# Sums over the rows of w_ada on TensorE, with the weights stationary, in one layer of a hybrid decoder

## The chip, the core and the metric

The kernel runs on one core of one Trainium2 chip. The metric is the device time of one execution in microseconds (us), the median of several runs.

## What is computed

One layer of a decoder trunk on a sequence of 1024 tokens of 1024 channels, conditioned by a vector c. From c come six vectors of 1024 (shift, scale and gate, for the mixing part and for the feed-forward part), and they are what the change is about:

```python
c_act = jax.nn.silu(c)
ada = c_act @ w_ada[l] + b_ada[l]                  # (1024) @ (1024 x 6144)
sh_m, sc_m, g_m, sh_f, sc_f, g_f = jnp.split(ada, 6, axis=-1)
h = modulate(rms_norm(x), sh_m, sc_m)              # h * (1 + sc) + sh
proj = h @ w_in[l]                                 # z for RWKV-7, u for S5
...
x = x + g_m[:, None, :] * mix                      # after the output projection
h = modulate(rms_norm(x), sh_f, sc_f)
ffn = (jax.nn.silu(h @ ffn_w_gate[l]) * (h @ ffn_w_up[l])) @ ffn_w_down[l]
x = x + g_f[:, None, :] * ffn
```

w_ada has 1024 rows and 6144 columns in float32, 25 MB. Everything is float32; large products are made as three products of a high and a low part (float32r).

## The kernel before

Channels lie on the 128 partitions, tokens on the free axis. The engines are TensorE (PE, with its weight loads, PEld), VectorE (DVE), ScalarE (ACT) and GpSimd (POOL); nearly all loads and stores are issued by SyncE (SP) from one queue. The program is written as generators that are woven into each other, and a scheduler then sets the order of the instructions on each engine from a model of their times, so that an edit can move instructions that it does not touch. Within an engine, and within SP's queue, the order is fixed: an instruction that waits holds back those behind it.

The stages, with their times in the profile: the startup (0 to 106 us), in which x is normalized, transposed by products with diagonals (`ptr`, `transpose_x`, L337), modulated (`hT`, `modulate`, L346) and multiplied by the columns of w_in for u (`pu`, `u_mm`, L363); the rest of the input projection (`pz`), the S5 recurrence and the preparation of RWKV (to about 440 us); the RWKV recurrence in chunks (`p`, `chunk`, L1037) woven with the gate of S5 (`pglu`, `s5_glu`, L763) and the triangular solve (`solve`, L980); the output projection of the first half of the tokens (`po`, `outproj`, L1271), to about 662 us; then the feed-forward network (`pgate`, `pup`, `pdn`, `ffn`, L1343) by halves, woven with what is left of RWKV.

The six vectors are made in blocks of 128 columns. `cact` holds silu(c) as eight columns, one for each block of 128 rows of w_ada. `ada_load` (L278) loads the 1024 rows of n blocks of columns in four tiles `wada`, each with two blocks of rows. `ada_acc` (L287) makes a running sum `acc` over the eight blocks of rows, elementwise: a product with the scalar `cact[:, 0]` (L293), then seven multiply-adds on DVE (L295), or, for some pieces, a product on ACT (L297) and a sum on POOL (L298). What is left is a sum over the partitions, and `ada_cols` (L301) makes it with one product for each block of columns, weights `acc`, one moving column of ones (`pac<-ones,acc`, L304), and then adds b_ada into `mod` (L305).

- Parts 0 and 1 (shift and scale of the mixing part) are made in the startup, in two halves of four blocks of columns (L528 to L557): the first half before the channels 0 to 511 are modulated, the second before the channels 512 to 1023.
- Parts 2 and 3 are made by `ada_steps` (L816, `adg`, L1239) in eight pieces of two blocks beside the recurrence and the gate of S5; every second piece has its sums on ACT and POOL.
- Parts 4 and 5 are made in eight pieces (`adl`, L1417), all on DVE, beside the output projection. The norm of the feed-forward part (`norm_f`, L1316) needs parts 3 and 4, the gate row (`bcast_gate`, L1245) part 5.

## Time and profile before

| | us |
|---|---|
| median of 3 runs | 1602.5 |
| lowest, highest | 1602.16, 1603.44 |
| span of the profiled execution | 1598.3 |

The profile's page gives the profiled execution's span, from its first to its last instruction, and no other time of it; the median of the runs stands 4.2 us above the span.

How to read it: the page gives the busy time of each engine and its share of the span, then the span in 40 slices with the busy tenths and TensorE's granted clock (in tenths of full speed; full is 2.4 GHz, one half of it 1.2 GHz, and a slice's figure is the mean over it). A chain of waits leads back from the last instruction; its shares tell which work stood on the path. Groups of instructions have their count, their busy time, the mean of one, and the idle time of the engine before them with what ended it. A float32 product appears as two records of PE and two weight loads.

### The profile page before, as it was taken

What the parts mean: (1) busy time and instruction counts of PE and PEld (TensorE: products, weight loads), DVE (VectorE), ACT (ScalarE), POOL (GpSimd) and SP (SyncE); (2) the same over time, 40 slices, a digit from 0 to 9 for tenths busy, and PEclk for the clock granted to TensorE, in tenths of its full rate; (3) what the DMA queues carried; (4) which work ended last, traced back from release to release, by engine and by line L of the source; (5) the groups of instructions that cost most, each with busy time, mean ns of one, the idle gap of its engine ahead of it and who ended that gap; (6) DMA issues with size and microseconds to landing.
All of it is one profiled execution on the core that took longest, in us unless ns stands there. A gap on an engine that the chain in (4) does not pass through costs nothing.

```text
span 1598.3 us, 23239 instructions
## 1 busy us (share of the span) xinstructions
PE 1416.4 (89%) x9167; PEld 1146.8 (72%) x9167; DVE 988.7 (62%) x1687; ACT 551.9 (35%) x881; POOL 540.9 (34%) x452
## 2 busy tenths in 40 slices
PE   3897798897958878698999999899997999999997
PEld 3675576776747756576777777677786888888885
DVE  5959458889686889854448855345626433433335
ACT  4341234344245653233225422224443222222223
POOL 4358344443053333145000003400251254444543
PEclk9897999999878989799999999899999999999999
DMA  9424674353454356353223224422831433232331
GB/s 277 146 79 143 171 233 152 109 134 100 93 161 129 122 177 196 115 116 97 66 67 113 86 88 106 97 68 68 222 104 50 137 93 105 81 105 92 99 99 53
DMA packets 266220, 189.78 MB, mean 119 GB/s; under 512 B 71670, under 2 KB 237184, under 8 KB 266112
## 3 DMA queue, kind: packets, MB, share of 16 engines
q1 hardware_dynamic: 264624, 186.65, 39.7%
q8 instruction: 72, 1.18, 0.3%
q0 software_dynamic: 816, 0.57, 0.2%
q10 hardware_dynamic: 672, 1.08, 0.2%
q14 instruction: 36, 0.29, 0.1%
HBM read 159.20 MB, written 31.16 MB: 119 GB/s over the span
## 4 chain that ended last, share of the span: by engine, by line
PE 56%; DVE 22%; DMA 8%; issue 5%; POOL 5%; ACT 2%; SPq 2%; DVEq 0%; POOLq 0%; ACTq 0%
PE pup L268 14%; PE pgate L268 13%; PE pdn L268 13%; PE pz L268 3%; DMA wada<-in_w_ada_dram 3%; PE p L1051 3%; DVE acc L295 2%; POOL XU L997 2%; POOL stmp L995 2%; PE pu L365 2%; PE po L1303 2%; DVE zo L864 1%; DVE stmp L995 1%; PE pA L951 1%; DVE XU L997 1%
## 5 line engine op out<-in xcount | busy, mean ns | idle before, releaser
L268 PE MATMUL pdn<-wd,act 128*128 128x512 f32 x1056 | 269.1, 397 | 0.7 <-DVE x L1352 0.6
L268 PE MATMUL pup<-h,hl_up 128*128 128x512 f32 x1056 | 268.6, 397 | 0.2 <-ACT hl_up L131 0.2
L268 PE MATMUL pgate<-h,hl_g 128*128 128x512 f32 x1056 | 264.1, 396 | 1.2 <-ACT hl_g L131 1.2
L1352 DVE TENSOR_TENSOR x<-pdn,x 128x512 f32<-128x512 f32 x176 | 119.0, 688 | 185.8 <-PE pdn L268 185.2
L268 PEld LDWEIGHTS pup<-h,hl_up 128*128 128x128 f32 x1056 | 198.1, 189 | 45.9 <-issue 2.6
L268 PEld LDWEIGHTS pdn<-wd,act 128*128 128x128 f32 x1056 | 196.6, 189 | 47.4 <-DVE x L1352 2.1
L268 PEld LDWEIGHTS pgate<-h,hl_g 128*128 128x128 f32 x1056 | 196.6, 188 | 47.4 <-issue 3.6
L268 PE MATMUL pz<-hT,hl_z 128*128 128x256 f32 (+1 forms) x1008 | 184.7, 340 | 37.0 <-ACT zt L859 20.8
L268 PEld LDWEIGHTS pz<-hT,hl_z 128*128 128x128 f32 x1008 | 154.7, 202 | 63.6 <-ACT zt L859 25.5
L1387 DVE TENSOR_TENSOR rawd<-rawd,gfb 128x1024 f32<-128x1024 f32 x44 | 54.9, 1248 | 101.2 <-DMA rawd<-in_ffn_w_down_dram 80.5
L1303 PE MATMUL po<-wo,yhl 128*128 128x512 f32 x384 | 99.1, 412 | 3.7 <-ACT wo L131 1.5
L131 ACT CAST hl_up<-raw_up 128x1024 fp32r<-128x1024 f32 x44 | 46.2, 1051 | 129.3 <-PE pup L268 110.2
L1303 PEld LDWEIGHTS po<-wo,yhl 128*128 128x128 f32 x384 | 74.6, 198 | 22.4 <-ACT wo L131 2.2
L131 ACT CAST wd<-rawd 128x1024 fp32r<-128x1024 f32 x44 | 45.7, 1049 | 117.6 <-DVE rawd L1387 86.8
L863 POOL TENSOR_TENSOR zo<-zt 128x512 f32<-128x512 f32 x28 | 40.9, 1461 | 109.9 <-ACT zt L859 107.2
L295 DVE SCALAR_TENSOR_TENSOR acc<-wada,cact,acc 128x256 f32<-128x256 f32 (+1 forms) x112 | 71.3, 644 | 5.4 <-DMA wada<-in_w_ada_dram 4.1
L127 POOL TENSOR_TENSOR yhl<-yt,yhl 128x512 fp32r<-128x512 f32 x16 | 23.9, 1494 | 149.4 <-ACT yhl L1288 144.1
L127 POOL TENSOR_TENSOR hl_g<-raw_g,hl_g 128x1024 fp32r<-128x1024 f32 x19 | 45.7, 2407 | 81.3 <-ACT hl_g L131 73.0
L1381 ACT ACTIVATE sgt<-pgate 128x512 f32<-128x512 f32 x44 | 26.4, 599 | 133.9 <-PE pgate L268 133.8
L995 POOL TENSOR_TENSOR stmp<-LU,XU 128x126 f32<-128x126 f32 (+22 forms) x62 | 28.0, 451 | 129.3 <-DMA LU<-l_d 124.6
L127 POOL TENSOR_TENSOR wd<-rawd,wd 128x1024 fp32r<-128x1024 f32 x19 | 50.4, 2654 | 54.6 <-ACT wd L131 54.6
L127 POOL TENSOR_TENSOR hl_up<-raw_up,hl_up 128x1024 fp32r<-128x1024 f32 x19 | 50.8, 2676 | 51.7 <-ACT hl_up L131 51.7
(372 smaller groups left out, 2453.6 us busy)
## 6 DMA issues: line engine op xcount, KB each, us to landing
raw_g<-in_ffn_w_gate_dram SPq DMA_DIRECT2D x44, 512.0 KB, 3.7
raw_up<-in_ffn_w_up_dram SPq DMA_DIRECT2D x44, 512.0 KB, 3.8
rawd<-in_ffn_w_down_dram SPq DMA_DIRECT2D x44, 512.0 KB, 3.5
wada<-in_w_ada_dram SPq DMA_DIRECT2D x64, 256.0 KB, 3.2
raw_z<-in_w_in_dram SPq DMA_DIRECT2D x28, 512.0 KB, 4.2
wada<-in_w_ada_dram SPq DMA_DIRECT2D x16, 512.0 KB, 7.9
wraw<-in_w_out_dram SPq DMA_DIRECT2D x32, 256.0 KB, 4.1
zt_d<-zo SPq DMA_DIRECT2D x28, 256.0 KB, 2.3
```

What stands on the lines that cost most here:

```text
L127: (eng or G).tensor_tensor(out=out, in0=a, in1=b, op=ALU.subtract)
L131: S.copy(dst[:, 0], src)
L268: PE.matmul(ps, lhsT=lf(a, k), rhs=rf(b, k), start=(n == 0), stop=(n == 3 * kb - 1))
L295: V.scalar_tensor_tensor(out=acc, in0=wt, scalar=cact[:, k:k + 1], in1=acc, op0=ALU.mult, op1=ALU.add)
L365: PE.matmul(pu[hf, b], lhsT=uw[b][:, a_, k, :], rhs=hT[hf, k][:, b_, :], start=(k == 0 and n == 0), stop=(k == 7 and n == 2))
L863: G.tensor_tensor(out=o, in0=zt[:, 0:HT], in1=zt[:, 1:HT + 1], op=ALU.subtract)
L995: SOLVE.tensor_tensor(out=t, in0=LU[:, j, j + 1:32].unsqueeze(2).to_broadcast([P, nt, nk]), in1=X[:, j:j + 1, 0:nk].to_broadcast([P, nt, n ...
L997: SOLVE.tensor_tensor(out=X[:, j + 1:32, 0:nk], in0=X[:, j + 1:32, 0:nk], in1=t, op=ALU.add)
L1051: PE.matmul(ps[r, h], lhsT=a, rhs=b, start=(n == 0), stop=(n == len(ops) - 1))
L1303: PE.matmul(pss[i], lhsT=yh[k][:, a, 128 * i:128 * i + 128], rhs=wo[:, b], start=(k == 4 and n == 0), stop=(k == 3 and n == 2))
L1352: V.tensor_tensor(out=t, in0=ps, in1=t, op=ALU.add)
L1387: V.tensor_tensor(out=raw, in0=raw, in1=gfb, op=ALU.mult)
```

## The change

The running sums go. `ada_mm` multiplies the tiles of w_ada as they are: each block of 128 x 128 is the stationary operand, the moving operand is one column of `cact`, so that a block of columns takes eight products where it took one. Two products (one tile) accumulate in a column of PSUM; the four columns of the four tiles are added by a reduction on DVE in `ada_out`, which then adds b_ada. The tiles' buffers go from 6 (startup) and 4 to 8 each. In the startup the first half is now written behind the transposes and the loads of w_in, the second half where it was. `ada_steps` lags one piece behind its loads where it lagged two behind its sums.

```diff
-    def ada_acc(pl, wts, n, eng=V):
-        """silu(c) times the weights, summed over the blocks of rows"""
-        acc = pl.tile([P, 128 * n], F32, tag="acc", bufs=2 if n > 2 else 3, name="acc")
-        for k in range(8):
-            wt = wts[k // 2][:, k % 2, :]
-            if k == 0:
-                V.tensor_scalar_mul(acc, wt, cact[:, 0:1])
-            elif eng is V:
-                V.scalar_tensor_tensor(out=acc, in0=wt, scalar=cact[:, k:k + 1], in1=acc, op0=ALU.mult, op1=ALU.add)
-            else:
-                S.mul(wt, wt, cact[:, k:k + 1])
-                G.tensor_tensor(out=acc, in0=acc, in1=wt, op=ALU.add)
-        return acc
-
-    def ada_cols(acc, part, j0, n, ps):
-        for j in range(n):
-            PE.matmul(ps[:, j:j + 1], lhsT=acc[:, 128 * j:128 * j + 128], rhs=ones[:, 0:1], start=True, stop=True)
-        V.scalar_tensor_tensor(out=mod[:, part, j0:j0 + n], in0=ps, scalar=1.0 if part in (1, 4) else 0.0,
+    def ada_mm(wts, part, j0, n, ps):
+        for kk in range(4):
+            for j in range(n):
+                for k in range(2):
+                    PE.matmul(ps[:, n * kk + j:n * kk + j + 1], lhsT=wts[kk][:, k, 128 * j:128 * j + 128],
+                              rhs=cact[:, 2 * kk + k:2 * kk + k + 1], start=(k == 0), stop=(k == 1))
+
+    def ada_out(part, j0, n, ps):
+        m = mod[:, part, j0:j0 + n]
+        V.tensor_reduce(m, ps[:, 0:4 * n].rearrange("p (k j) -> p j k", k=4), axis=mybir.AxisListType.X, op=ALU.add)
+        V.scalar_tensor_tensor(out=m, in0=m, scalar=1.0 if part in (1, 4) else 0.0,
                                in1=col("b_ada", 8 * part + j0, n), op0=ALU.add, op1=ALU.add)
...
-    def mods(a0, a1, j0):
-        ada_cols(a0, 0, j0, 4, pac[:, 256 + j0:260 + j0])
-        ada_cols(a1, 1, j0, 4, pac[:, 264 + j0:268 + j0])
+    def mods(ws, j0):
+        for part in range(2):
+            ada_mm(ws[part], part, j0, 4, pac[:, 256 + 16 * part:272 + 16 * part])
+            ada_out(part, j0, 4, pac[:, 256 + 16 * part:272 + 16 * part])
...
-    wa = [ada_load(sp, part, 0, 4, 6) for part in range(2)]
+    wa = [ada_load(sp, part, 0, 4, 8) for part in range(2)]
     dgs = norm_x(0, xts[0])
-    acs = [ada_acc(sp, w, 4) for w in wa]
     transpose_x(xts[0], dgs)
     uw += [load_u(0), load_u(1)]
+    mods(wa, 0)
     xts.append(load_x(1))
-    wa = [ada_load(sp, part, 4, 4, 6) for part in range(2)]
-    mods(*acs, 0)
+    wa = [ada_load(sp, part, 4, 4, 8) for part in range(2)]
...
-    acs = [ada_acc(sp, w, 4) for w in wa]
...
-    mods(*acs, 4)
+    mods(wa, 4)
...
-    def ada_steps(pl, parts, ps, mix=lambda j: j % 4):
+    def ada_steps(pl, parts, ps):
         todo = []
         def cols():
-            acc, part, j = todo.pop(0)
-            ada_cols(acc, part, j, 2, ps("pac2")[:, 0:2])
+            w, part, j = todo.pop(0)
+            o = ps("pac2")
+            ada_mm(w, part, j, 2, o)
+            ada_out(part, j, 2, o)
         for part in parts:
             for j in (0, 2, 4, 6):
-                todo.append((ada_acc(pl, ada_load(pl, part, j, 2, 4), 2, V if mix(j) else None), part, j))
-                if len(todo) > 2:
+                todo.append((ada_load(pl, part, j, 2, 8), part, j))
+                if len(todo) > 1:
                     cols()
                 yield
```

The scheduler orders the engines anew. Three places on PE follow, each before and after; the names are those of the program (`pac` the sums for the six vectors, `ptr` transposes of x, `pu` products for u, each with its count behind an x).

The first is the startup. Before, from PE's second instruction on, down to the first products for u:

```order
L342 MATMUL ptr<-dg,xt 128x128 x16
L304 MATMUL pac<-ones,acc 128x1 x4
L342 MATMUL ptr<-dg,xt 128x128 x28
L304 MATMUL pac<-ones,acc 128x1 x4
L342 MATMUL ptr<-dg,xt 128x128 x12
L365 MATMUL pu<-hT_98,hl_u 128x512 x2
```

The same place of the change, and after the "..." the second half of the startup:

```order
L293 MATMUL pac<-cact,wada 128x1 x8
L336 MATMUL ptr<-dg,xt 128x128 x12
L293 MATMUL pac<-cact,wada 128x1 x6
L336 MATMUL ptr<-dg,xt 128x128 x12
L293 MATMUL pac<-cact,wada 128x1 x5
L336 MATMUL ptr<-dg,xt 128x128 x8
L293 MATMUL pac<-cact,wada 128x1 x45
L336 MATMUL ptr<-dg,xt 128x128 x12
...
L360 MATMUL pu<-hT_109,hl_u 128x512 x3
L293 MATMUL pac<-cact,wada 128x1 x64
L210 MATMUL pac<-ident,rows_943 128x128
L360 MATMUL pu<-hT_102,hl_u 128x512 x8
```

Sixteen products became 128: 64 among the first transposes, with 45 of them in a row, and 64 in a row ahead of the products for u that need the second half (`hT_102` on).

The second is the middle, the first piece of part 2 among the products of the recurrence (`p`), of the gate of S5 (`pglu`) and of the solve (`pO`). Before:

```order
L1051 MATMUL p_4339<-U,tm 64x64 x2
L1051 MATMUL p_4411<-ak,tm 64x64
L1027 MATMUL pO<-VT,GT 32x32 x32
L304 MATMUL pac_4246<-ones,acc 128x1 x2
L268 MATMUL pglu<-zhl,hl_glu 128x256 x12
```

In the change, the first two pieces:

```order
L268 MATMUL pglu<-zhl,hl_glu 128x256
L293 MATMUL pac_4223<-cact,wada 128x1 x16
L1046 MATMUL p_4253<-ST,ar 64x64
...
L1022 MATMUL pO<-VT,GT 32x32 x32
L293 MATMUL pac_4304<-cact,wada 128x1 x16
L1046 MATMUL p_4159<-ak,tm 64x64 x2
```

Each piece is a burst of 16 products in one place where it was two.

The third is the end of the conditioning, after the output projection (`po`). Before:

```order
L1303 MATMUL po<-wo,yhl 128x512 x45
L304 MATMUL pac_5862<-ones,acc 128x1 x2
L1303 MATMUL po<-wo,yhl 128x512 x24
L304 MATMUL pac_5883<-ones,acc 128x1 x2
L304 MATMUL pac_5904<-ones,acc 128x1 x2
L304 MATMUL pac_5908<-ones,acc 128x1 x2
L304 MATMUL pac_5912<-ones,acc 128x1 x2
L938 MATMUL pb<-rz,blk 128x512
```

In the change:

```order
L293 MATMUL pac_5891<-cact,wada 128x1 x8
L1298 MATMUL po<-wo,yhl 128x512 x4
L293 MATMUL pac_5891<-cact,wada 128x1 x4
L1298 MATMUL po<-wo,yhl 128x512 x56
L293 MATMUL pac_5891<-cact,wada 128x1 x4
L293 MATMUL pac_5918<-cact,wada 128x1 x16
L293 MATMUL pac_5945<-cact,wada 128x1 x16
L293 MATMUL pac_5972<-cact,wada 128x1 x16
L293 MATMUL pac_5999<-cact,wada 128x1 x16
L293 MATMUL pac_6026<-cact,wada 128x1 x16
L293 MATMUL pac_6045<-cact,wada 128x1 x16
L933 MATMUL pb<-rz,blk 128x512
```

After the last `po` eight small products became a hundred in a row; a piece of 16 and the rest of the second stand among the `po` ahead of it.

## Rows read from the trace of the kernel before

**Rows 1.** The page: busy time of TensorE, and its granted clock in 40 slices.

```profile
PE 1416.4 (89%) x9167; PEld 1146.8 (72%) x9167; DVE 988.7 (62%) x1687; ACT 551.9 (35%) x881; POOL 540.9 (34%) x452
...
PEclk9897999999878989799999999899999999999999
```

**Rows 2.** Stretches: length, then busy PE, PEld, DVE, ACT, POOL, clock, DMA, GB/s.

```profile
0.00:106.00 106.00, 73.12 (x359) 62.48 (x359) 70.06 (x206) 48.08 (x71) 38.06 (x43) 0.92 0.61 184
...
440.00:562.00 122.00, 92.76 (x1262) 78.06 (x1258) 99.72 (x238) 62.51 (x133) 53.42 (x65) 0.83 0.46 136
...
590.00:646.30 56.30, 49.51 (x208) 38.50 (x209) 53.31 (x88) 17.31 (x31) 25.70 (x20) 0.94 0.60 191
646.30:661.60 15.30, 3.37 (x18) 3.09 (x16) 13.57 (x37) 4.14 (x10) 0.00 (x0) 0.59 0.56 175
661.60:1598.00 936.40, 896.79 (x5162) 720.21 (x5162) 466.33 (x672) 288.67 (x421) 265.81 (x229) 0.98 0.33 95
```

**Rows 3.** Chain of waits, shares by line, 440 to 562 us.

```profile
by line: DMA wada<-in_w_ada_dram 10.6%; DVE XU L997 10.3%; PE pglu L268 10.0%; PE p L1051 9.2%; DVE stmp L995 7.8%; issue 4.0%; DVE acc L295 3.8%; DVE ST L1065 3.8%; DVE acc L293 3.2%; DMA VT<-x_d 2.8%; DVE zz L810 2.5%; DVE lrs L252 2.3%; 
```

**Rows 4.** Chain of waits, shares by line, 562 to 662 us.

```profile
by line: DVE acc L295 23.7%; issue 8.4%; DMA wada<-in_w_ada_dram 6.1%; DVE lrs L1103 5.5%; DMA wraw<-in_w_out_dram 4.3%; DVE lrs L1104 3.7%; DVE ta L930 3.2%; DVE yo L1311 3.0%; DVE acc L293 2.8%; DVE rz L935 2.6%; ACT L892 2.6%; DVE x L131
```

**Rows 5.** PE in order of time, 18 to 110 us: start, length, line, records behind x.

```profile
18.26 6.85 PE L342 MATMUL ptr<-dg,xt 128*128 128x128 f32 x32 [8.24 <-DVE dg L333]
24.95 0.95 PE L304 MATMUL pac<-ones,acc 128*128 128x1 f32 x8
25.77 3.82 PE L342 MATMUL ptr<-dg,xt 128*128 128x128 f32 x32
...
63.17 10.04 PE L365 MATMUL pu<-hT,hl_u 128*128 128x512 f32 x43 [0.59 <-DVE hT L127]
73.05 0.95 PE L304 MATMUL pac<-ones,acc 128*128 128x1 f32 x8
...
78.59 26.54 PE L365 MATMUL pu<-hT,hl_u 128*128 128x512 f32 x108 [0.37 <-ACT hT L349]
```

**Rows 6.** DVE in order of time, startup: silu(c) and the last part of `mod`.

```profile
15.27 0.17 DVE L316 TENSOR_TENSOR cact<-cact,cols 128x8 f32<-128x8 f32 x1 [1.35 <-ACT cact L315]
...
77.54 0.15 DVE L305 SCALAR_TENSOR_TENSOR mod<-pac,cols 128x4 f32<-128x4 f32 x1
```

**Rows 7.** Instructions of `acc`: the one-column products, ns least/median/most, first and last start.

```profile
L304 PE MATMUL pac<-ones,acc x96: 164/250/372, 25.0 to 661.0; 128*128 128x1 f32 x96
```

**Rows 8.** PE in order of time, 646 to 661.5 us.

```profile
650.66 1.01 PE L304 MATMUL pac<-ones,acc 128*128 128x1 f32 x4 [3.98 <-DVE mod L305]
657.78 0.98 PE L304 MATMUL pac<-ones,acc 128*128 128x1 f32 x4 [6.11 <-DVE acc L295]
```

**Rows 9.** The stretch 650 to 661 us, columns as in rows 2.

```profile
650.00:661.00 11.00, 2.64 (x12) 2.53 (x12) 10.21 (x29) 3.56 (x10) 0.00 (x0) 0.50 0.51 159
```

**Rows 10.** Two stretches around 495.4 us, columns as in rows 2.

```profile
492.00:495.40 3.40, 2.87 (x90) 2.47 (x88) 3.20 (x10) 1.93 (x4) 0.00 (x0) 1.00 0.00 0
495.40:498.80 3.40, 2.63 (x12) 2.63 (x12) 2.55 (x6) 2.47 (x7) 0.85 (x1) 0.50 0.48 159
```

**Rows 11.** PE in order of time, 491.9 to 495.5 us.

```profile
491.65 0.75 PE L268 MATMUL pglu<-zhl,hl_glu 128*128 128x256 f32 x5
...
493.06 1.20 PE L1027 MATMUL pO<-VT,GT 32*32 32x32 f32 x64
494.31 0.61 PE L304 MATMUL pac<-ones,acc 128*128 128x1 f32 x4
```

**Rows 12.** ScalarE in order of time, 77 to 84 us.

```profile
77.73 5.75 ACT L349 ACTIVATE hT<-xt,mod 128x512 fp32r<-128x512 f32 x8 [8.84 <-DVE mod L305]
```

**Rows 13.** Groups by line, 440 to 562 us: busy us, mean ns of one, idle before.

```profile
L298 POOL TENSOR_TENSOR acc<-acc,wada 128x256 f32<-128x256 f32 x28 | 22.2, 791 | 9.3 <-ACT ssum L796 7.8 <-PE p L1051 0.3 <-DVE acc L293 0.3
L295 DVE SCALAR_TENSOR_TENSOR acc<-wada,cact,acc 128x256 f32<-128x256 f32 x28 | 15.3, 547 | 0.8 <-DMA wada<-in_w_ada_dram 0.4
```

**Rows 14.** A stretch with dense transfers, columns as in rows 2.

```profile
575.00:580.00 5.00, 3.64 (x8) 1.31 (x6) 3.33 (x5) 4.94 (x6) 0.00 (x0) 0.73 1.07 319
```

**Rows 15.** Groups by line, 590 to 661.6 us, columns as in rows 13.

```profile
L295 DVE SCALAR_TENSOR_TENSOR acc<-wada,cact,acc 128x256 f32<-128x256 f32 x56 | 34.2, 623 | 1.1 <-DMA wada<-in_w_ada_dram 0.5
```

More of the change, by code (lines that the diff above doesn't have):

```diff
@@ L1416 @@
     das = ExitStack()
-    adl = ada_steps(pool("adp3", stack=das, side="right"), (4, 5), ps_a, lambda j: True)
+    adl = ada_steps(pool("adp3", stack=das, side="right"), (4, 5), ps_a)
     weave((LIM(late, 16), 2), o0, (LIM(adl, 2), 1))
```

## Prediction

> **What bounds the kernel now.** I read the page first. TensorE (PE) is busy for 89% of the span, and its granted clock stands between 0.7 and 1.0 in the forty slices [rows 1]: little room for more work on PE. The table by stage shows where that room is [rows 2]: 33 us in the first 106 us, 29 us between 440 and 562, 7 us between 590 and 646, 12 of 15 us between 646 and 662, and only 40 of 936 us in the feed-forward network after that. What the change can win or lose lies ahead of 662 us; a shift there goes to the end one to one. VectorE (DVE) is the fuller engine from 590 to 662 (53.3 of 56.3 us and 13.6 of 15.3 us).
>
> The chain of waits says what the sums cost there today. Between 440 and 562 it gives 10.6% to loads of w_ada and 7.0% to the DVE sums, so 12.9 + 8.5 = 21.5 us of 122 [rows 3]; between 562 and 662 the sums on DVE alone have 26.5% of 100 us [rows 4]. In the startup the second pair of small products runs at 73.05 us, its part of `mod` is written at 77.54 us, and 108 products for u follow it in 26.54 us [rows 5, 6].
>
> **Price of a one-column product.** The trace holds 48 of them, each recorded as two weight loads and two matmuls, 96 records [rows 7]. Eight records go from 24.95 to the next start at 25.77 us: 0.82/8 = 0.10 us a record, 0.205 us a product. The 128-column products behind them cost 0.12 us a record (3.82/32; 0.21 in the 32 ahead, which begin after 8 idle us), so the weight load sets the pace, not the column [rows 5]. Between 650 and 661 us the granted clock is 0.50, the lower level (1.2 GHz), and four records take 1.01 us [rows 8, 9]; less the 0.37 us of the last one (the longest such record, [rows 7]) that is 0.213 us a record, 0.43 us a product. The change makes 384 products in place of 48.
>
> What the trust in either price hangs on is the clock in a long run of them, which the trace does not have. The nearest row: from 492.0 to 495.4 us PE was busy for 2.87 of 3.40 us, with products of 64 and 32 columns and at last four one-column records, and the clock stood at 0.50 in the next 3.4 us [rows 10, 11]. Busy, but with narrow products, PE lost the upper level (2.4 GHz) some 3 us after its last wide product. A run of one-column products is narrower still. So I take it that a long run goes at 0.205 us for its first 3.1 us (15 products) and at 0.43 us afterwards; the bound from below is 0.205 us throughout.
>
> The Trainium skill ("TensorE: Matmul & The Clock Gate", section on LDWEIGHTS) puts a weight load at its columns over 1.2 GHz, 107 ns for 128, with no word of the clock gate. By that a product would cost about 0.21 us at either level and the sum would be that of rival B below; the records at 0.213 us under clock 0.50 speak against it.
>
> **Startup (0 to 106 us).** The weights are stationary for 4 x 32 = 128 products here in place of 16; 64 of them stand in one run just ahead of the second half of the modulation, and 45 of the first 64 in a run too. DVE loses 28 sums and 4 products with a scalar. In the order PE has nothing ahead of the second `mod` that can hide them: from 15.45 us, when `cact` is written [rows 6], it must do 128 x 0.205 = 26.2; 128 transpose records at 0.12 = 15.4, of which the first 24 are as slow as now (32 in 6.85 us, +2.3) [rows 5]; eight products still at the lower clock, +1.8; 84 products for u at 10.04/43 = 0.23 = 19.3; two parameter transposes 0.8; and stalls as now, 2.0. That ends at 83.2 us. Two small DVE operations (0.15 each, as the one that writes `mod` now; the added reduction is bounded by it) and one ScalarE operation (5.75/8 = 0.72) [rows 12] give 84.3, and 108 products at 0.23 end at 109.1 against 105.13: **+4.0**. The second half of w_ada is loaded long before its run, so its eight tiles at once cost nothing; SP holds x back by two loads, which the PE queue covers. With the clock falling, 30 of the run of 45 and 49 of the run of 64 cost 0.225 more, 17.8; after each run the clock has to rise again, as today's 24 transposes (+2.3) and the 108 products (26.54 - 24.8 = 1.7) show: **+25.8** in all.
>
> **Middle (440 to 562 us).** Eight bursts of 16 in place of eight of two: 112 x 0.205 = 23.0 us on PE, in which PE queues the recurrence (`p`) and the gate of S5 (`pglu`) behind each burst, and behind its wait for the load. They also hold the one PSUM bank of tag s for longer. Away go 28 sums on DVE (15.3 us) and as many on GpSimd (22.2 us), with ScalarE's products before them [rows 13]. All of the 23 us hidden in PE's 29 idle us and the whole 21.5 us of chain gone would be -21.5; nothing hidden and nothing gone +23.0. I take the middle, half of each: +11.5 - 10.7 = **+0.8**. With the slower clock a burst of 3.3 us seldom falls by itself; a quarter of 112 x 0.225 = 6.3 makes it **+7.1**. SP now holds the writes of the triangular solve behind loads that wait for PE; I take nothing for that.
>
> **End of the conditioning (590 to 662 us).** Of 128 products 28 stand among those of the output projection, and 100 come in one unbroken run after its last: nothing else lies there for PE, and the norm, the gates and the first gate product wait for it. At 0.205 the run is 20.5 us; its loads, 24 of 256 KB at 319 GB/s (the rate of 575 to 580 us), need 20 us, so they bind no more than PE [rows 14]. With the clock falling it is 15 x 0.205 + 85 x 0.43 = 39.6 us. In its place go the 15.3 us from 646.3 to 661.6 in which DVE finished its sums: **+24.3** (or **+5.2**). Before 646 the relief of DVE (34.2 us of sums, [rows 15]) can give PE back at most its 6.8 idle us, against 20 more products (4.1 us): taken as nothing.
>
> **Sum.** 25.8 + 7.1 + 24.3 = 57.2 us on a span of 1598.3: 1655.5. The page gives no other time of the profiled execution than its span; the median of the runs, 1602.5, lies 4.2 above, and 1655.5 + 4.2 = **1659.7 us**.
>
> **Rivals.** *B, the clock stays up.* Then 4.0 + 0.8 + 5.2 = +10.0, 1612.5 us. For it: at 25.77 us the transposes went on at 0.12 after eight one-column records [rows 5], and PE is never idle in the runs. Against it: the busy stretch that lost the level [rows 10]. The Trainium skill (same page, "What's actually happening") says the clock follows how busy PE has been, by which an unbroken run would be B's case; the busy 2.87 of 3.40 us ahead of a fall do not agree.
>
> *C, faster.* The relief decides: all 23 us of the middle lie in PE's 29 idle us and all 21.5 us of sums and loads leave the chain; the projection gains its whole 6.8 us, and the clock holds: 4.0 - 21.5 + 5.2 - 6.8 = -19.1, 1583 us. It turns the sign once the middle gains more than 9.2 us (2.4 if the projection gains its 6.8) with the clock up. For it: DVE is on the chain there. Against it: the run of 100 and that of 64 have no cover, and the bursts sit in front of a recurrence that PE and DVE hand back and forth.
>
> *D, nothing moves.* The loads of w_ada, not the sums, are what is waited for; PE waits in DVE's place, and the cost of B goes against a part of the relief: about 1603.
>
> **How the numbers follow.** My forecast with its falling clock has 0.69, B 0.20, C 0.06, D 0.04; 0.01 is left. The upper end of the forecast is the middle with all bursts on the path, two thirds of them at the lower clock: 23 + 17 - 10.7 = 29 in place of 7, about 1680. The low end is B less 3 us, 1610. Between them lie most of the forecast and more than half of B; what is left out is C, D, the lower part of B and a tail above. Inside 0.2% (3.2 us, about what the measurement tells from no change) there is 0.04, below it 0.06, above it 0.90.
>
> **What would show it.** Right: one-column records at 0.2 us with granted clock 0.5 late in the runs of 64 and 100; the first u product after the second `mod` near 104 us (84 in B); about 40 us between the last `po` and the first product behind the run. Wrong in size: clock 1.0 in both runs and records at 0.10 us (B). Wrong in sign: the middle ending some 20 us after its start earlier than now, and PE idle between the bursts (C).

## The result, and the profile after

The changed kernel takes 1691.5 us (median of 4 runs, 1688.0 to 1692.0) against 1602.3 us before: ratio 1.0539, 95% interval 1.0506 to 1.0572. That is 89 us slower, on the side that was forecast, and 11 us above the upper end of the range.

The first lines of the page of the changed kernel (span; PE's busy time, share and records; granted clock in 40 slices; rows 1 has those of before):

```profile
span 1689.5 us, 24359 instructions
PE 1537.4 (91%) x9839; PEld 1268.9 (75%) x9839; DVE 902.7 (53%) x1575; ACT 539.2 (32%) x851; POOL 511.8 (30%) x424
PEclk8878999999887787959999999999998999999999
```

PE has 121 us more of work than before and DVE 86 us less: the relief came, but the time grew. To see where the 91 us of span come from, both executions are cut at the same events: the first `pz`; the last `pz`; the first `pd` (the product that begins the closing steps of a quarter of the recurrence) behind the first and behind the second quarter, the latter called "the recurrence's end" below; the last `po` of the first half of the tokens; the end of the conditioning. The table by stage of the kernel before, up to the last `po` (stretch, its length, then busy us and instructions of PE, PEld, DVE, ACT, POOL, granted clock, DMA share, GB/s; the two stretches behind it are in [rows 2]):

```profile
0.00:106.20 106.20, 73.12 (x359) 62.48 (x359) 70.26 (x206) 48.27 (x71) 38.06 (x43) 0.92 0.61 184
106.20:428.10 321.90, 270.76 (x1850) 223.29 (x1851) 257.27 (x393) 106.11 (x173) 150.12 (x87) 0.92 0.46 137
428.10:514.30 86.20, 60.91 (x921) 52.33 (x919) 63.32 (x155) 40.27 (x94) 38.62 (x53) 0.76 0.58 145
514.30:568.10 53.80, 45.11 (x611) 37.45 (x610) 48.77 (x113) 30.03 (x59) 18.20 (x19) 0.90 0.39 124
568.10:646.30 78.20, 66.35 (x254) 47.95 (x255) 69.21 (x116) 34.46 (x54) 30.11 (x22) 0.91 0.61 190
```

The same for the changed kernel, to the end:

```profile
0.00:130.40 130.40, 113.92 (x584) 104.37 (x584) 44.21 (x178) 49.05 (x71) 36.19 (x43) 0.82 0.49 150
130.40:452.00 321.60, 269.68 (x1850) 222.35 (x1851) 257.35 (x393) 105.95 (x172) 150.43 (x87) 0.93 0.46 137
452.00:567.40 115.40, 98.73 (x1151) 90.44 (x1149) 53.59 (x157) 39.18 (x85) 27.24 (x36) 0.75 0.53 139
567.40:635.40 68.00, 56.62 (x655) 45.45 (x654) 30.00 (x77) 27.78 (x48) 16.05 (x13) 0.87 0.38 111
635.40:713.50 78.10, 61.98 (x247) 45.90 (x245) 44.39 (x75) 24.62 (x44) 18.09 (x16) 0.80 0.33 105
713.50:756.60 43.10, 41.29 (x202) 40.49 (x201) 7.68 (x30) 4.14 (x10) 0.00 (x0) 0.54 0.39 116
756.60:1689.50 932.90, 895.20 (x5162) 719.92 (x5160) 465.49 (x670) 288.48 (x421) 263.82 (x229) 0.98 0.34 96
```

Startup 106.2 to 130.4: +24.2. From `pz` to `pz`: nothing. The recurrence and the gate of S5, 140.0 (86.2 + 53.8) to 183.4: **+43.4**. The output projection behind them, 78.2 to 78.1: nothing. The end, 15.3 to 43.1: +27.8. The feed-forward network, 936.7 to 932.9: -3.8. Forecast were +25.8, 0, +7.1, 0, +24.3 and 0: five of the six stages within 4 us, the middle off by 36.

Two of these stages do not hold the same work as before. In the new order a quarter of the projection's 192 records stands ahead of the recurrence's end, where none stood:

```profile
L1298 PE MATMUL po<-wo,yhl 128*128 128x512 f32 x48 | 14.0, 439 | 2.7 <-ACT yhl L1283 1.8 <-POOL yhl L127 0.9
```

So the +43.4 could in part be the projection's, and the projection took as long as before with 14.0 us less of its own work. The run e10_midorder below settles the first: without a `po` in the middle, the stage is still 39.8 us longer.

The second half of the startup on PE (start, duration, line, operation and count):

```profile
67.11 9.36 PE L360 MATMUL pu<-hT,hl_u 128*128 128x512 f32 x40
76.31 11.29 PE L293 MATMUL pac<-cact,wada 128*128 128x1 f32 x64
87.86 13.81 PE L293 MATMUL pac<-cact,wada 128*128 128x1 f32 x64 [0.27 <-DVE mod L298]
102.98 22.21 PE L360 MATMUL pu<-hT,hl_u 128*128 128x512 f32 x90 [0.56 <-ACT hT L343]
```

and the table of this run by stretches (the clock is the last figure but two):

```profile
76.30:79.30 3.00, 3.00 (x27) 2.99 (x26) 0.00 (x0) 0.00 (x0) 0.00 (x0) 0.93 0.00 0
79.30:87.00 7.70, 7.70 (x37) 7.70 (x38) 0.00 (x0) 0.00 (x0) 0.00 (x0) 0.50 0.00 0
88.00:101.50 13.50, 13.50 (x64) 13.50 (x64) 0.00 (x1) 0.00 (x0) 0.00 (x0) 0.50 0.01 1
```

Nothing but the conditioning runs on PE for 25 us, busy without a gap, and some 3 us into it the granted clock falls to the lower level (1.2 GHz); the last 64 records take 13.81/64 = 0.216 us each. The first u product behind it starts at 102.98 us; 104 was forecast for the slow clock, 84 for the fast one. The end looks the same:

```profile
713.46 0.95 PE L293 MATMUL pac<-cact,wada 128*128 128x1 f32 x8
719.66 6.99 PE L293 MATMUL pac<-cact,wada 128*128 128x1 f32 x32 [0.26 <-DVE mod L298]
755.90 2.07 PE L933 MATMUL pb<-rz,blk 128*128 128x512 f32 x2 [0.26 <-DVE mod L298]
```

42.4 us lie between the last `po` and the first product behind the run (about 40 were forecast). A burst of 16 products (32 records) takes 6.99 us, 0.437 us a product, and 0.26 us of waiting for the column of `mod` stand in front of each. In the middle the bursts have both prices:

```profile
543.95 6.98 PE L293 MATMUL pac<-cact,wada 128*128 128x1 f32 x32 [2.06 <-ACT sg L787]
558.51 3.73 PE L293 MATMUL pac<-cact,wada 128*128 128x1 f32 x32
```

3.73/16 = 0.233 us a product at best (0.205 was forecast). All 128 products there keep PE busy for 36.5 us, 32 us more than the 16 products of before.

### The profile page after: what moved, and what is told of

Its sections match the earlier page's. It is cut to its first block, busy times and chain, and to the rows that moved or that the text cites. A ratio compares the mean times of both kernels' runs of the same rounds, so it can differ in the third digit from the quotient of the medians.

```text
span 1689.5 us, 24359 instructions
## 1 busy us (share of the span) xinstructions
PE 1537.4 (91%) x9839; PEld 1268.9 (75%) x9839; DVE 902.7 (53%) x1575; ACT 539.2 (32%) x851; POOL 511.8 (30%) x424
## 4 chain that ended last, share of the span: by engine, by line
PE 69%; DVE 13%; DMA 7%; POOL 4%; issue 3%; ACT 2%; SPq 1%; DVEq 0%; POOLq 0%; ACTq 0%
PE pup L268 13%; PE pgate L268 13%; PE pdn L268 12%; PE pac L293 7%; PE po L1298 5%; PE pz L268 4%; PE p L1046 3%; PE pu L360 3%; POOL XU L992 2%; POOL stmp L990 2%; PE pglu L268 2%; PE pA L946 1%; DVE zo L859 1%; DVE f L729 1%; DMA XU<-x_d 1%
## 5 line engine op out<-in xcount | busy, mean ns | idle before, releaser
L293 PE MATMUL pac<-cact,wada 128*128 128x1 f32 x768 | 132.1, 306 | 8.1 <-DMA wada<-in_w_ada_dram 4.0
L293 PEld LDWEIGHTS pac<-cact,wada 128*128 128x128 f32 x768 | 131.3, 269 | 10.3 <-DVE cact L310 4.2
L858 POOL TENSOR_TENSOR zo<-zt 128x512 f32<-128x512 f32 x28 | 41.3, 1477 | 108.9 <-ACT zt L854 106.2
L127 POOL TENSOR_TENSOR yhl<-yt,yhl 128x512 fp32r<-128x512 f32 x16 | 23.1, 1449 | 166.2 <-ACT yhl L1283 130.4
L1376 ACT ACTIVATE sgt<-pgate 128x512 f32<-128x512 f32 x44 | 26.3, 598 | 129.4 <-PE pgate L268 129.2
```

The lines of the kernel that those rows point to most:

```text
L127: (eng or G).tensor_tensor(out=out, in0=a, in1=b, op=ALU.subtract)
L293: PE.matmul(ps[:, n * kk + j:n * kk + j + 1], lhsT=wts[kk][:, k, 128 * j:128 * j + 128], rhs=cact[:, 2 * kk + k:2 * kk + k + 1], start=(k ...
L858: G.tensor_tensor(out=o, in0=zt[:, 0:HT], in1=zt[:, 1:HT + 1], op=ALU.subtract)
```

## The experiments

Times are medians, differences (+) are to the median of the kernel before in the same job; kernels of different jobs are compared by these or by the spans of their profiled executions. The runs of the kernel before lie between 1597 and 1608 us over all jobs, and most kernels here have two runs, so that a difference of 5 us or less between two of them tells little. Dates of the events, from the order of time on PE (us; in brackets the difference to before):

| kernel | last u product | recurrence's end | last `po` of half 1 | span |
|---|---|---|---|---|
| before | 105.1 | 568.1 | 646.3 | 1598.3 |
| changed | 129.3 (+24) | 635.4 (+67) | 713.6 (+67) | 1689.5 (+91) |
| e1_startup | 129.2 (+24) | 602.9 (+35) | 688.2 (+42) | 1645.8 (+48) |
| e2_middle | 104.2 (-1) | 613.0 (+45) | 692.8 (+46) | 1645.4 (+47) |
| e3_end | 103.5 (-2) | 567.1 (-1) | 647.6 (+1) | 1628.2 (+30) |
| e4_few | 92.5 (-13) | 547.8 (-20) | 627.2 (-19) | 1571.3 (-27) |
| e10_midorder | 104.0 (-1) | 609.8 (+42) | 688.9 (+43) | 1644.1 (+46) |

### Which place loses it

Three kernels take over one place each.

```diff
+    mods(wa, 0) ... mods(wa, 4)                        # e1_startup: parts 0, 1
+    adg = ada_steps_n(pool("adp2", ...), (2, 3), ps_s) # e2_middle: the changed kernel's pieces
+    adl = ada_steps_n(pool("adp3", ...), (4, 5), ps_a) # e3_end
```

> The new products in the startup alone; the other two places keep their running sums. Theory (the loss is PE time at the slow record price, place by place, and adds up): the last u product, 105.13 us before and 128.9 + 0.4 us with the whole change, ends near 129, and everything behind it is shifted: 1602 + 24 = 1626 us. Rival 1 (the forecast's terms): +25.8, 1628 us, the same within its uncertainty, so this run tests the sign and size of that term only. Rival 2 (the cost lies in the new order of the whole program and not in a place): between 1602 and 1610, or over 1640.

1644.8 us, +44.5. The u products end where expected (129.2), but the span grows by twice as much: another 24 us are lost behind the startup, in code that is the same as before. So the theory's shift is there, but its time is missed by 19 us, and rival 2's bound (over 1640) is met; which part is order is taken up below.

> The new products in the middle alone (parts 2 and 3 of the modulation). Theory (PE is full there, so the eight bursts of 3.7 to 7.0 us go onto the recurrence's path whole, and the relief of DVE is worth little): +40, since with the whole change the recurrence's last pd product moved from 572.8 to 638.4 us, 65.6 us, of which the startup brought 24: 1643 us. Rival (the forecast's term, half hidden and half of the relief gained): +7.1, 1610 us; the other 33 us would then be made by the end of the conditioning, whose pieces are woven with the recurrence.

1647.9 us, +47.6: the theory's place and size. The loss is made in the middle and passed on unchanged by the end.

> The new products at the end of the conditioning alone (parts 4 and 5). Theory (only the unbroken run costs, 42.4 us in place of 15.3): +27, 1629 us, with the last product of the output projection still near 646 us. Rival (the end also holds up the output projection, the 35 us by which first to last product of it grew): +60, 1662 us, with its last product near 680 us.

1632.8 us, +32.5, with the last `po` at 647.6 us: the run behind it is the whole cost, as the theory has it (44.9 us from there to the first product behind the run, 15.3 before: 29.6 of the 30 us of span).

Added up the three make 125 us, the whole change 89: what the places cost is not a sum.

### Products or relief

```diff
-        for kk in range(4): for j in range(n): for k in range(2): PE.matmul(...)
+        for j in range(n): PE.matmul(... wts[3][:, 1, ...], cact[:, 7:8] ...)      # e4_few
+        for kk in range(2): for j in range(n): for k in range(2): PE.matmul(...)   # e5_midhalf
-        for j in range(n):
+        for j in [j for j in range(n) for _ in range(times)]:                      # e6_midadd: ada_cols of before, times=8
```

> The whole change, but with one product a block in place of eight: 48 one-column products as before, all loads, buffers, the order of the pieces and the relief of the other engines kept; seven eighths of the sum over the rows of w_ada are left out, and the sum of the four partial columns is a copy. Theory (the cost is the 336 more products on PE): the 89 us are gone, and what the relief is worth shows: between 1575 and 1602 us. Rival (the cost comes with the order of loads and pieces, or with waits for w_ada): 1640 us or more.

1573.8 us, -26.4, just below the theory's range. With as few products as before (the sum is then incomplete) the change is a gain of 26 us: 13 in the startup, 13 more by the end of the recurrence (and 6 lost on the way), the rest at the end. The change's loads and buffers are all in this kernel, so they are not what costs; with the 336 added products come 89 + 26 = 115 us, which is their own time, what the clock loses by them and the order that the scheduler makes for them.

> The middle alone as in e2_middle (1647.9 us, +47.6), but with four products a block in place of eight: half of the sum over the rows of w_ada is left out in parts 2 and 3; loads, buffers and the relief of DVE, ScalarE and GpSimd are the same. Theory (each of the 128 products costs its whole time on the recurrence's path, and the relief is worth a fixed gain): the 128 product records that go were worth about 16 us of the 31.5 that the bursts took, so 1632 us or less. Rival (the cost is the new order, or the loads that PE now waits for, and not the products): within 6 us of e2_middle.

1624.3 us, +21.4. Half of the products take away 26 of the 47.6 us (21 by the spans), 0.3 to 0.4 us for each of the 64, though PE was busy with them for only 0.26 us (32.4 us for 256 records in e2_middle, 16.0 us for 128 here). So a product in the middle seems to cost the program more than its own time; the surplus over the 16.4 us of busy time that went is 4 us by the spans and 10 by the medians, near the scatter of the runs.

> The kernel before with its running sums kept everywhere, but in the middle each one-column product is made eight times over (128 products in place of 16 there): the added PE work without the relief. Theory (PE work is the cost, and the relief is worth some 7 to 14 us in the middle): +47.6 plus that, 1655 to 1662 us. Rival 1 (the relief is worth nothing because PE is the bound there): 1648 us as e2_middle. Rival 2 (the forecast's idea that half of the products hide in PE's idle time): +15, 1615 us, and the middle's loss in e2_middle is then one of loads and buffers.

1670.9 us, +68.0, more than the theory allowed. Against e2_middle the sums that are kept cost 20 us (23 by the spans). Not all of this need be the relief: in e6_midadd one of the `po` that stand ahead of the recurrence's end makes PE wait 7.1 us for `yhl`, which none does in e2_middle. Less that wait 13 to 16 us are left (an estimate from these two traces), close to the 13 of e4_few and no less than the 10.7 that were forecast. The products without the relief cost 68 us, twice what they added to PE's busy time (36.6 us, 4.8 before).

### Order

Each edit makes the scheduler order the program anew. Two ways of holding it: e7_midpin queues the output projection behind the recurrence on PE (and is written so that the two are no longer woven); e9 to e13 queue PE's products by a table of the order before.

```diff
+        if half == 0 and dh == 0 and k == 4 and n == 0: behind(m, pdl[1, 1])       # e7_midpin
...
+    PE = InOrder(tc, nc.tensor)      # e9_startpin, e10_midorder, e11_allorder, e12_halforder, e13_poolorder
+        for made in (self.made.get((PE_FROM[f], c + i)) for i in range(n)):
+            self.tc.add_manual_dep(made.ins, last.ins.name, NoSync ...); last = made
```

> e2_middle with one thing more: the first product of the output projection is queued on PE behind the last pd product of the first half's recurrence, where it stood in the kernel before; in e2_middle 48 records of it (14.0 us) stand ahead of the recurrence's end. Theory (those 14 us are a second part of the loss: the order made for the program puts them where the recurrence waits, and they shorten nothing behind it): pd ends 14 us earlier, and the time is 1634 us. Rival (they fill time in which the recurrence waits anyway): 1648 us or more.

1641.5 us, +38.7, by the spans 8 us less than e2_middle; the recurrence ends at 609.2 in place of 613.0 us. Between the two theories: 4 of the 14 us were in the recurrence's way, the others filled time in which it waited. They gained nothing behind it either: the projection, with all of its records, takes 75.0 us here and 79.8 us in e2_middle with a quarter of them gone.

> e1_startup with one thing more: behind the startup, all 6684 products are queued on PE in just the order of the kernel before (edges of order only, no waits). Theory (the startup itself costs 24 us, and the other 24 us of e1_startup's span are the new order that was made for the rest of the program): 1626 us, every date behind the startup shifted by 24. Rival (the 24 us are work: a lower level of the clock or later loads that the startup's lateness brings): 1640 us or more.

1633.1 us, +30.0, by the spans 14 us less than e1_startup. The last `pz` and the first `pglu` are now shifted by 24 and 25 us, near what they should, the recurrence's end by 34. So 14 of the 24 us behind the startup were PE's order; the other 10 appear between the first `pglu` and the end of the recurrence's first quarter, with PE's order the same. From the last `pz` to there (427.8 to 514.3 us before, 452.1 to 547.7 here) PE is busy for 68.3 in place of 61.2 us with the same products, at a lower clock (0.68 in place of 0.76), and the products `pG` wait for their loads (`XU`) for 9.0 in place of 3.1 us, while other waits shrink. Why the loads come later stays open; the order on the other engines and in SP's queue was not held.

> e2_middle with all of its 6940 other products queued on PE in the order of the kernel before; only the eight bursts are placed freely, and land within a few products of where the small products stood. Theory 1 (half of the middle's loss is order): 1620 to 1628 us, the second pd at 590 us. Theory 2 (it is all work: 27 us of added products on the path and nothing gained): 1640 us or more. The forecast's term would be 1610 us.

1643.9 us, +40.8: theory 2. With PE's order that of before, the middle costs nearly as much as in e2_middle (1 us less by the spans, 7 by the medians), so most of it is work. No `po` stands ahead of the recurrence's end, and the products other than the bursts stand in the old order, so the books can be kept. Both are cut at the first `pss` product, which in the kernel before stands just ahead of the first small products of the middle. Before:

```profile
428.10:485.80 57.70, 35.72 (x469) 30.36 (x467) 44.75 (x111) 26.04 (x63) 27.43 (x39) 0.70 0.63 159
485.80:568.10 82.30, 70.31 (x1063) 59.42 (x1062) 67.35 (x157) 44.26 (x90) 29.39 (x32) 0.90 0.42 122
```

The same of e10_midorder:

```profile
430.00:483.60 53.60, 38.84 (x501) 34.44 (x498) 36.27 (x105) 20.32 (x49) 17.46 (x25) 0.78 0.69 158
483.60:609.80 126.20, 112.43 (x1257) 97.84 (x1255) 52.44 (x144) 39.08 (x76) 16.46 (x18) 0.72 0.33 103
```

PE idle: 22.0 + 12.0 = 34.0 us before, 14.8 + 13.8 = 28.5 now. Two thirds of the idle time that was to hide the bursts lies in the first stretch, where one of the eight stands; beside the other seven it did not shrink. PE busy: 106.0 to 151.3, +45.3. The costliest groups on PE in this stage, before (busy us, mean ns of one, idle time ahead of them):

```profile
L268 PE MATMUL pglu<-zhl,hl_glu 128*128 128x256 f32 x192 | 37.2, 356 | 9.7 <-ACT sg L794 7.3 <-ACT zhl L131 1.9 <-POOL hl_glu L127 0.5
L1051 PE MATMUL p<-tm 64*64 64x64 f32 x128 | 10.4, 248 | 1.4 <-DVE U L1060 1.4
L304 PE MATMUL pac<-ones,acc 128*128 128x1 f32 x32 | 4.8, 254 | 1.4 <-ACT sg L794 1.3
```

and in e10_midorder (the line is that of the helper that queues by the table):

```profile
L124 PE MATMUL pglu<-zhl,hl_glu 128*128 128x256 f32 x192 | 40.2, 377 | 2.3 <-ACT zhl L245 2.2
L124 PE MATMUL p<-tm 64*64 64x64 f32 x128 | 12.0, 274 | 6.0 <-DVE U L1208 6.0
L124 PE MATMUL pac<-cact,wada 128*128 128x1 f32 x256 | 36.3, 276 | 2.7 <-ACT sg L923 2.7
```

The small products take 36.3 - 4.8 = 31.5 of the 45.3 us. The other 14 are the same products as before, slower one by one (356 to 377 ns, 248 to 274), with the granted clock down from 0.90 to 0.72 in the second stretch. That it is the clock shows when the records are told apart by the level at their start: a record of `pglu` takes 299 ns at the upper and 423 ns at the lower level before, 301 and 427 ns here, but 115 of the 192 start at the lower level where 89 did; of the 992 records of `p` (222 and 316 ns before, 224 and 315 here) it is 430 where it was 230. 31.5 + 13.8 - 5.5 = 39.8 us, the length that was added (179.8 - 140.0).

> The whole change with the products queued on PE in the order of the kernel before up to the end of the first half's output projection; the one-column products, the transposes and u products of the startup, and the preparation of the third quarter are left free. Theory (order is a part of the 89 us): startup 24, run at the end 27 and the middle as e10_midorder shows it, without a further loss: 1602 + 51 + 20 = 1673 us or less. Rival (all is work): 1688 us or more.

1697.7 us, +94.6, by the spans 6.5 us more than the changed kernel: the rival. For the whole change the order that the scheduler makes is no worse than the old one as far as PE goes; PE's order explains none of the 89 us.

### Clock and form of the products

```diff
+            u_mm(hf, k, b)                                            # e8_startmix: one k, three records
+            for part, kk, j, k2 in [small.pop(0) for _ in range(6)]:  # then six small products
...
-    PE.matmul(ps[:, ...], lhsT=wts[kk][:, k, 128 * j:128 * j + 128], rhs=cact[:, ...])  # e14_endmove
+    PE.matmul(o[0:1, 0:256], lhsT=cact[:, k:k + 1], rhs=w[k // 2][:, k % 2, :], start=(k == 0), stop=(k == 7))
+    S.copy(row[0:1, :], o[0:1, 0:256])
+    PE.matmul(o[:, 256 + jj:257 + jj], lhsT=row[0:1, 128 * jj:128 * jj + 128], rhs=ones[0:1, 0:1], ...)
```

> The startup alone as in e1_startup (1644.8 us), but the second 64 of its products stand in clumps of four to six among the u products, three 512-column records between clumps, in place of one run of 128 records (25.1 us with a granted clock of 0.50 for most of it). Theory (narrow products alone lose the upper level, and records at the upper level take 0.117 us): the 64 take 15 us, the last u product ends near 119 in place of 129.2 us, and the time is 1635 us. Rival (a record costs 0.2 us whatever stands around it, by waits for its weights and not by the clock): 129 us and 1645 us.

1634.0 us, +31.1, the theory's time, and yet the theory is wrong: the last u product ends at 133.3 us, 4 later than in e1_startup and 14 later than the theory had it. PE in order of time:

```profile
75.95 1.39 PE L581 MATMUL pac<-cact,wada 128*128 128x1 f32 x12
77.21 0.94 PE L385 MATMUL pu<-hT,hl_u 128*128 128x512 f32 x3
80.45 2.55 PE L581 MATMUL pac<-cact,wada 128*128 128x1 f32 x12
82.87 1.63 PE L385 MATMUL pu<-hT,hl_u 128*128 128x512 f32 x3
```

and by stretches:

```profile
73.00:79.20 6.20, 6.20 (x48) 5.81 (x46) 0.00 (x0) 0.00 (x0) 0.00 (x0) 1.00 0.01 3
79.20:106.90 27.70, 27.43 (x106) 24.94 (x106) 0.67 (x4) 0.84 (x2) 0.00 (x0) 0.51 0.00 1
```

The clock falls in spite of three records of 512 columns after every twelve small ones, only later, and then the wide records pay too (0.94 to 1.63 us for three). The time came out lower because only 6 us are lost behind the startup, where e1_startup loses 24. The right time was luck, and only the dates on PE told it from a success.

> The end alone, as e3_end (+30), but turned round: a column of cact is stationary and 256 columns of w_ada move, eight products a piece, with a copy of the row by ScalarE and two products of one row that turn it into columns. Theory (the price of the change's form is a weight load of 128 columns for one column of work, and the clock falls for want of wide products): 16 records of 256 columns at 0.26 us, as pg has them at the upper level, 4.2 us a piece in place of 7.0; seven pieces behind the last product of the output projection take 33 us with their copies, and the time is 1620 us. Rival (the clock falls here as well, and a record of 256 columns takes 0.45 us at the lower level): 7.2 us a piece and more with the copies, 1632 us or more.

1620.7 us, +19.6 against +32.5 (6 us less by the spans): the theory's time, and in the run about its prices (3.61 us for the products of a piece, 4.2 expected). The end by stretches in e3_end (weights stationary), and its burst:

```profile
656.00:692.00 36.00, 34.93 (x160) 34.51 (x160) 1.47 (x9) 1.04 (x1) 0.00 (x0) 0.50 0.37 111
663.28 6.99 PE L314 MATMUL pac<-cact,wada 128*128 128x1 f32 x32 [0.26 <-DVE mod L319]
```

and in e14_endmove (weights moving):

```profile
657.00:687.00 30.00, 25.07 (x121) 10.50 (x120) 5.37 (x17) 5.20 (x16) 0.00 (x0) 1.00 0.52 158
662.46 3.61 PE L854 MATMUL pac<-wada,cact 128*1 128x256 f32 x16 [0.29 <-DVE mod L859]
666.53 0.60 PE L858 MATMUL pac<-ones,row 1*128 1x1 f32 x4 [0.45 <-ACT row L856]
```

A piece takes 5.0 us from start to start in place of 7.25, with the waits for ScalarE's row and DVE in it, and the clock stays at the upper level although PE is less busy. The run is 31.1 us long in place of 44.9 (656.4 to 687.6, 647.4 to 692.3); a part of this is lost again, since the last `po` comes 9 us later than in e3_end, in a new order. In the startup and the middle the matrix was not tried as the moving operand.

The Trainium skill ("TensorE: Matmul & The Clock Gate", section "What's actually happening") lets the clock follow how busy PE has been. If busy is what the profile's rows call busy, these two do not agree with it: 34.93 of 36.00 us busy at 0.50, 25.07 of 30.00 us busy at 1.00.

### A version that beats both

None did. Four edits of the kernel before were tried, two of them a second time with PE's order held (e12_halforder, e13_poolorder).

```diff
+    wa = [ada_load(sp, part, 0, 4, 7) ...]; mods_n(wa, 0)  # c1_half: first half as products
-    adl = ada_steps(..., (4, 5), ps_a, lambda j: True)
+    adl = ada_steps(..., (4, 5), ps_a)                     # b_mixend, and in c5_pool
-    ada_load(pl, part, j, 2, 4)
+    ada_load(pl, part, j, 2, 8 if part > 3 else 4)         # c3b_buf8
+    adg = ada_steps(..., (2, 3), ps_s, lambda j: False)    # c5_pool
```

> A mixture of the two kernels in the startup alone: the first half of its conditioning by one-column products (they fall into a stretch in which PE waits for x and the weights), the second half by running sums on DVE as before, seven buffers for the loads. Theory (PE work costs only where PE has nothing to wait for; DVE, freed of 14 sums and two products with a scalar, gets to the second half's sums earlier): the second part of mod is written before 70 us in place of 77.5, the last u product ends some 8 us earlier than 105.1, and the time is 1590 to 1596 us if the rest keeps its order. Rival (the first 64 products hold up the transposes, the lower level that follows them is carried into the u products, and DVE's sums wait for the loads): u ends at 110 us or later, 1607 us or more.

1629.1 us, ratio 1.0168 (1.0150 to 1.0186). The rival's time, and in the startup nearer to the rival than to the theory: PE does wait there, but the 64 products lose the clock (64 records in 13.82 us from 33.98 us on), the u products end at 108.3 us, 3 later than before, and 26 us more are lost behind them.

> c1_half with all products behind the startup queued in the order of the kernel before. Theory (c1_half lost 3 us in the startup and 26 us by order): 1606 us. Rival (the loss behind the startup is work): 1625 us or more.

1617.7 us, ratio 1.0092 (1.0063 to 1.0122): PE's order was 12 of those 26 us by the spans. The result lies between the two theories, and the rest stays open.

> The kernel before with a quarter of the pieces at the end of the conditioning (two of eight) summed by ScalarE and GpSimd in place of DVE, as its middle has it. Theory (at the end the sums on DVE are the bound: 13.6 of the last 15.3 us): mod is done some 4 us earlier, 1597 to 1599 us. Rival (the bound there is the loads and their four buffers, or GpSimd's sums of 0.8 us are themselves last): 1602 us or more.

1605.1 us, ratio 1.0009 (0.9995 to 1.0023). No difference that can be told; the theory's gain is missed. The edit moves more than its expectation says: four of the eight pieces at the end, not two, go to ScalarE and GpSimd (56 sums on GpSimd in the whole kernel in place of 28).

> The kernel before with eight buffers in place of four for the loads of w_ada at the end of the conditioning, the one edit of the change there that is not a product. Theory (the loads land when they are needed; DVE's sums are the bound): no change, 1600 to 1604 us, so none of the loss of the change comes from the buffers. Rival (the last loads, issued at 654.9 us for want of a free buffer, set the end): 6 us less, 1596 us, and then the change's own gain from its buffers was swallowed by its run of products.

1605.6 us against 1603.5 in this job, ratio 1.0014 (0.9998 to 1.0029): no change, as the theory has it. These buffers are no part of the loss.

> The kernel before with all eight pieces of the middle summed by ScalarE and GpSimd (four of them before), and two of eight at the end: relief of DVE with no work for PE. Theory (the relief of DVE is what gives the 27 us of e4_few where PE pays nothing): the 14 further sums on GpSimd cost 0.8 us each on an engine that is busy for 53 of the middle's 122 us, and the middle gets 4 to 10 us shorter, 1592 to 1598 us. Rival (ScalarE and GpSimd are themselves part of the chain there, or share the path to memory with DVE): 1602 us or more.

1623.9 us, ratio 1.0136 (1.0115 to 1.0157): the rival. Here too the end has four of its eight pieces moved, and the sums on GpSimd go from 28 to 84, so 56 are added and not 14: the test loads GpSimd far more than its theory had reckoned with.

> c5_pool (1623.9 us, +20) with all products but the conditioning's queued on PE in the order of the kernel before. Theory (its loss is the new order; the relief of DVE is worth 4 to 10 us): 1594 to 1602 us. Rival (the 0.8 us sums on GpSimd, or ScalarE's products before them, come late and are waited for): 1612 us or more.

1615.0 us, ratio 1.0078 (1.0035 to 1.0121). About seven of the 20 us were PE's order; the time of the rest is the rival's. With 84 sums on GpSimd the 26 us that e4_few shows are not to be had; a smaller share for GpSimd was tried at the end alone (b_mixend).

## Why the prediction was wrong in size

**Price of a product: right at the lower level, a little low at the upper.** 0.43 us at the lower level was forecast, 0.437 measured; 0.205 at the upper, 0.233 in the bursts of the middle.

**The clock: right, and the choice that decided the startup and the end.** The forecast let a long run go at the upper level for 3.1 us; the row has 0.93 for the first 3.0 us and 0.50 behind. Rival B (clock up, 1612.5 us) falls. The records of the products go at 0.117 us (3.73/32) at the upper and 0.218 us (6.99/32) at the lower level. The Trainium skill ("TensorE: Matmul & The Clock Gate", section "LDWEIGHTS") gives a load of 128 columns some 107 ns with no word of the level; the first of the two figures is near it, the second is not. [Rows 10, 11], in which a busy PE with narrow products had lost the level, were the right ones to trust.

**Startup: +25.8 forecast, +24.2 measured. End: +24.3 forecast, +27.8 measured** (its run 42.4 us against 39.6). **The feed-forward network: nothing, and -3.8. The stage of `po`: nothing, and nothing**, but here the exact number is luck: the stage has 48 of its records less than before and lasts as long, with the clock at 0.80 where it was 0.91; with all of its records in it, in e3_end, it is 2.3 us longer than before (567.1 to 647.6 us). The 4.2 us between span and median were 2.0 here (1691.5 against 1689.5).

**Middle: +7.1 forecast, +43.4 measured. This is the step that failed**: "I take the middle, half of each: +11.5 - 10.7". The second number held, on the low side: the relief is no smaller than that (about 13 us by e4_few, 13 to 20 by e6_midadd against e2_middle). The first was wrong by far: with the 6.3 us for the clock it puts 17.8 us of the products on the path, and they cost 68 us without relief (e6_midadd) and, with PE's order held, 39.8 us with it (e10_midorder), of which 31.5 are the products themselves and 13.8 the slower work around them, while PE's idle time gave 5.5. Three things were missed, and e10_midorder shows two of them by itself.

- PE's 29 idle us were taken as cover for the whole stage. They were a sum over two unlike stretches: 18.5 us of them lie ahead of 485.8 us (22.0 of 34.0 in the table above), and only one of the bursts stands there. The idle time beside the other seven did not shrink (12.0, then 13.8 us). A table by stage of the kernel before, cut at its first small product, shows this; the forecast's stood over the whole middle [rows 2].
- The clock was charged to the small products alone (6.3 us, a quarter of the bursts). It also slowed what stood around them: 13.8 us on the recurrence and the gate.
- The bursts stand in the queue of a recurrence that goes to and fro between PE and DVE. What this adds beyond the two above, and how much of it comes from the new order (8 us by e7_midpin, 1 by e10_midorder, both by the spans), is not taken apart; e6_midadd has 10 us more of idle time on PE than before, not less, and 7.1 of them are the wait of a `po` that the new order brought forward.

Because of this the upper end of the range was too low: its "all bursts on the path, two thirds at the lower clock" still took 10.7 us of relief off and charged the neighbours nothing.

**Rival C (faster) falls**, but its mechanism is real: e4_few has the gain (-26.4) as soon as the products are not paid for, 13 us of it in the startup, where rival C saw none. **Rival D falls**: if the loads of w_ada and not the sums were waited for, e4_few, which has the same loads, would not have gained.

## What to carry to other kernels

Idle time of the engine that is to take over work counts only in the stretch in which the work arrives: cut the table there before any of it is called cover. A matrix-vector product with the matrix stationary makes PE load 128 columns to move one; here it cost 0.23 us a block of 128 x 128, 0.44 in a run, and slowed the products around it, while the same sum with the matrix moving kept the upper level at the end of the conditioning, the one place where it was tried. Where a scheduler orders the program, compare dates of events as well as totals: an edit's total can be right for the wrong reason.

## What was not expected of the hardware and the program

- Wide records between narrow ones did not keep the upper level here: twelve one-column and three 512-column records in turn ran at 1.00 for 6.2 us and at 0.51 for the next 27.7 us (e8_startmix).
- PE less busy held the upper level: 25 of 30 us busy with 256 columns a record, granted clock 1.00, against 34.9 of 36.0 us busy with one column, 0.50 (e14_endmove, e3_end).
- An edit in the first 106 us cost 6 to 26 us behind it, in code that it does not touch (e8_startmix 6, e1_startup 24, c1_half 26, by the spans). Holding PE's order won back 14 and 12 us of the latter two, and lost 6.5 for the whole change (e11_allorder).
